# Attention with keys on the partitions: scores computed transposed, row minima from a separate product

## The chip, the cores and the metric

One core of a Trainium2 chip runs the kernel. TensorE (PE in the profile) multiplies matrices into PSUM, VectorE (DVE) and ScalarE (ACT) read PSUM and work elementwise, GpSimd (POOL) works elementwise on SBUF, and SyncE (SP) issues DMAs. Each engine takes its instructions in the order in which they were put in its queue, and waits on semaphores. The metric is the time of one execution on the device in microseconds (us): 4578.61 us is the median of three runs before the change (4577.62 to 4586.95 us).

## The reference, cut to what matters

Two layers. Each has a token mixer (two head groups in parallel: an RWKV-7 recurrence and multi-head latent attention) and a channel mixer. The change touches the attention alone: 8 heads, 1024 latent queries that read all 1280 keys, and, in the first layer only, 256 context queries that read the 256 context keys.

```python
def attend(q, k, v):                      # q, k: 96 features a head; v: 64
    s = jnp.einsum('bqhd,bkhd->bhqk', q, k).astype(F32) * (QK_DIM ** -0.5)
    p = jax.nn.softmax(s, axis=-1).astype(v.dtype)
    return jnp.einsum('bhqk,bkhd->bqhd', p, v)

def mla_latent_attention(q, k_lat, v_lat, k_ctx, v_ctx):
    k_all = jnp.concatenate([k_lat, k_ctx], axis=1)
    v_all = jnp.concatenate([v_lat, v_ctx], axis=1)
    ...
    ob = lax.map(lambda qi: attend(qi, k_all, v_all), qb)   # blocks of 128 queries
```

## The kernel before, in words

The program runs, for each of the two layers: input projections (`in_proj`), the token mixer (`mixer`), the output projection (`out_proj`) and the channel mixer (`ffn`). In the trace the mixers are the stretches from 695 to 1419 us and from 3026 to 3697 us. A Tile scheduler turns the code into one queue for each engine: code that is written earlier has priority, and what is not ready in its plan lets later work pass. So the queues interleave attention and recurrence. What runs on the chip is the fixed queue: an instruction that waits holds up all behind it on its engine.

`mixer` makes ten passes. Each emits a tenth of the attention work, then a chunk of the recurrence (`rwkv_seq` twice, `rwkv_inv2`, `rwkv_prep` for two passes ahead, `rwkv_out`). The recurrence is a chain PE, DVE or ACT, PE, DVE or ACT, with many small products (lines 871 to 1001), and a long run of small DVE instructions that invert triangular blocks (lines 912 and 913).

`attn(l, h, t, first)` computes two heads (h is a pair, e = 0 or 1 within it) for one tile of 128 queries (t). Queries are on the partitions. Its steps:

1. At the first tile of a pair, `raw` keys are loaded and split into a high and a low part (`ka`, lines 1036 and 1037). Each tile's queries are split the same way (`qa`, lines 1044 and 1045).
2. For each head, line 1062 makes the scores `sp` [128 queries, keys] in three PSUM tiles of 512, 512 and 256 keys, each from three products of parts (high x high, high x low, low x high). The tiles' tags s0, s1, s2 have one buffer each.
3. Line 1063 takes the minimum of each tile over the keys, line 1072 that of the three (the scores carry the opposite sign, so the minimum is softmax's maximum). Line 1075 makes P = exp(minimum - score) and its row sums with the accumulator. Lines 1082 and 1083 add the sums and invert them.
4. Keys must be on the partitions for the product with the values. So line 1094 transposes P in blocks of 128x128 into `tp` (four blocks, one buffer), DVE (line 1099) or ACT (line 1097) in turn copies `tp` to `pT`, and line 1104 multiplies with the values `va` into `av`: the two heads of the pair go to two halves of the output partitions. Both are fp32 products. A 128-key block of two heads takes two transposes and two products.
5. Line 1107 spreads the inverted sums over partitions by a product with the identity, and lines 1109 to 1111 scale `av` and store it.

PSUM has eight banks: three for `sp`, one each for `tp` and `av`, three for the recurrence.

## Time and profile before

| | |
|---|---|
| median of 3 runs | 4578.61 us (4577.62 to 4586.95) |
| the profiled execution, its own time | 4579.01 us |
| its span, first to last instruction | 4577.2 us |
| PE, DVE, ACT busy over the span | 4160.3, 2740.3, 1684.0 us |
| mixer of layer 0 (695 to 1419 us): PE, DVE, ACT busy | 635.98, 585.12, 370.07 of 724 us |
| mixer of layer 1 (3026 to 3697 us): PE, DVE, ACT busy | 591.82, 552.13, 337.88 of 671 us |
| granted clock of PE in the mixers; in a stretch of the channel mixer | 0.92 and 0.91; 1.00 |

A busy time is the union of the instructions' durations. A matmul's duration includes its way through the array, in which the next ones already stream, so the time that one costs in a stream is the distance between two starts in a timeline, not its duration. An fp32 matmul that is not a transpose stands in the trace as two instructions (two passes). The granted clock is the share of 2.4 GHz that the throttle let through; its other level is 1.2 GHz.

### The profile page before, as it was taken

The numbers are of one execution on the slowest core, as the hardware profiler recorded it, in microseconds if no ns is written. First come the engines' busy times: TensorE is split into PE (matmuls) and PEld (weight loads), VectorE is DVE, ScalarE is ACT, GpSimd is POOL, SyncE is SP. The second block draws the span as 40 slices with busy tenths as digits, with TensorE's granted clock in tenths as the row PEclk, the third lists the DMA queues.
The fourth block names the chain that finished last, engine by engine and source line by source line (L and its number), as shares of the span: only waits on it lengthen the run. The fifth ranks groups of instructions, "written<-read, shape, count | busy, mean of one in ns | idle before, by whom it ended". The sixth has DMA issues, their size and how long they took to land. (4 is left out here: it accounts for less than half of the span.)

```text
span 4577.2 us, 72936 instructions
## 1 busy us (share of the span) xinstructions
PE 4160.3 (91%) x29598; PEld 3301.1 (72%) x29598; DVE 2740.3 (60%) x4943; ACT 1684.0 (37%) x3000; POOL 543.2 (12%) x492
## 2 busy tenths in 40 slices
PE   8978888899988899999998979888989878999998
PEld 5756666677766788888886856666777656888887
DVE  3225567888886534444447235579888856555456
ACT  3203444544564431221223224464445534222222
POOL 1000000111223300000004000001111244000002
PEclk9989888998999999999998989889998889999999
DMA  6652334323333211111113222343222243111111
GB/s 219 242 174 94 104 120 123 87 66 78 82 77 129 93 39 35 40 40 33 47 35 107 86 72 106 111 142 78 61 72 71 68 135 125 55 51 51 42 51 65
DMA packets 425697, 401.36 MB, mean 88 GB/s; under 512 B 243472, under 2 KB 329936, under 8 KB 425360
## 3 DMA queue, kind: packets, MB, share of 16 engines
q1 hardware_dynamic: 425360, 396.69, 27.9%
q8 instruction: 233, 3.82, 0.3%
q14 instruction: 104, 0.85, 0.1%
HBM read 285.85 MB, written 110.72 MB: 87 GB/s over the span
## 5 line engine op out<-in xcount | busy, mean ns | idle before, releaser
L1266 PE MATMUL up<-u,hi 128*128 128x512 f32 (+1 forms) x3520 | 1012.3, 369 | 3.9 <-ACT hi L1256 3.9
L1266 PEld LDWEIGHTS up<-u,hi 128*128 128x128 f32 x3520 | 643.4, 189 | 119.6 <-ACT hi L1256 4.8
L1266 PE MATMUL up<-u,lo 128*128 128x512 f32 (+1 forms) x1760 | 648.3, 368 | 0.2
L297 PE MATMUL pj<-u,whi 128*128 128x512 f32 (+1 forms) x1888 | 565.9, 384 | 43.4 <-DVE o L318 38.3
L1313 DVE TENSOR_TENSOR acc<-dn,acc 128x512 f32<-128x512 f32 x340 | 233.2, 688 | 431.5 <-PE dn L1307 431.4
L297 PEld LDWEIGHTS pj<-u,whi 128*128 128x128 f32 x1888 | 352.5, 198 | 143.2 <-issue 48.3
L1266 PEld LDWEIGHTS up<-u,lo 128*128 128x128 f32 x1760 | 332.3, 189 | 58.5 <-DVE lo L1258 1.0
L297 PE MATMUL pj<-u,wlo 128*128 128x512 f32 (+1 forms) x944 | 363.5, 385 | 0.1
L1062 PE MATMUL sp<-ka,qa 96*128 96x512 f32 (+1 forms) x1200 | 318.8, 398 | 25.9 <-ACT P L1075 22.2
L1307 PE MATMUL dn<-hi,fh 128*128 128x512 f32 x792 | 311.5, 393 | 7.9 <-ACT fh L1281 4.0
L1256 ACT ACTIVATE hi<-raw 128x512 fp32r<-128x512 f32 x176 | 110.6, 630 | 563.8 <-PE up L1266 560.9
L1307 PE MATMUL dn<-lo,fh 128*128 128x512 f32 x792 | 309.8, 391 | 0.0
L1307 PE MATMUL dn<-hi,fl 128*128 128x512 f32 x792 | 305.6, 390 | 0.0
L1075 ACT ACTIVATE P<-sp,mx 128x512 f32<-128x512 f32 (+1 forms) x400 | 239.4, 606 | 146.3 <-DVE mx L1072 86.7
L1104 PE MATMUL av<-pT,va 128*64 128x128 f32 x2624 | 230.2, 299 | 59.7 <-DVE pT L1099 28.7
L1062 PEld LDWEIGHTS sp<-ka,qa 96*128 96x128 f32 x1200 | 214.6, 204 | 76.5 <-ACT P L1075 32.3
L1063 DVE TENSOR_REDUCE mx<-sp 128x1 f32<-128x512 f32 (+1 forms) x400 | 228.7, 586 | 36.7 <-PE sp L1062 34.7
L1094 PE MATMUL tp<-cst,P 128*128 128x128 f32 x1312 | 234.6, 301 | 7.8 <-ACT P L1075 4.4
L280 ACT ACTIVATE whi<-raw 128x512 fp32r<-128x512 f32 (+2 forms) x110 | 66.1, 603 | 471.7 <-PE pj L297 417.5
L1104 PEld LDWEIGHTS av<-pT,va 128*64 128x64 f32 x2624 | 149.8, 145 | 111.5 <-DVE pT L1099 30.4
L1258 DVE TENSOR_TENSOR lo<-raw,hi 128x512 fp32r<-128x512 f32 x176 | 125.3, 714 | 173.7 <-ACT hi L1256 161.2
L297 PEld LDWEIGHTS pj<-u,wlo 128*128 128x128 f32 x944 | 186.2, 197 | 41.5 <-issue 9.6
(254 smaller groups left out, 7253.5 us busy)
## 6 DMA issues: line engine op xcount, KB each, us to landing
wt<-in_w_ada_dram SPq DMA_DIRECT2D x96, 512.0 KB
raw<-in_w_up_dram SPq DMA_DIRECT2D x176, 256.0 KB
raw<-in_w_down_dram SPq DMA_DIRECT2D x88, 256.0 KB
raw<-in_w_in_dram SPq DMA_DIRECT2D x84, 256.0 KB
bkD<-lt SPq DMA_DIRECT2D x32, 640.0 KB
...
```

The costliest lines, as they stand in the source:

```text
L280: nc.scalar.activation(hi[:, :m], raw[:, :m], AF.Copy)
L297: nc.tensor.matmul(ps[:, o:o + n], ww, u[k][s], start=k == 0 and j == 0, stop=k == nk - 1 and j == 2)
L1062: nc.tensor.matmul(sp[:, o - b0:o - b0 + n], q[:, qq, e], A.k[e][:, kk, o:o + n], start=m == 0, stop=m == 2)
L1063: nc.vector.tensor_reduce(mx[:, i:i + 1], sp[:, :w], axis=AX.X, op=ALU.min)
L1075: nc.scalar.activation(P[:, o:o + w], sp[:, :w], AF.Exp, bias=mn, scale=-1.0, accum_out=mx[:, 4 + i:5 + i])
L1094: nc.tensor.transpose(tp[:, b, e], Ps[e][:, o:o + 128], self.ident)
L1104: nc.tensor.matmul(av[half[e], 0:128], A.v[:, k0 // 128 + kt, half[e]], pT[:, b, e], start=kt == 0, stop=kt == nkt - 1)
L1256: nc.scalar.activation(hi, raw, AF.Copy)
L1258: nc.vector.tensor_tensor(lo, raw, hi, op=ALU.subtract)
L1266: nc.tensor.matmul(ps[:, so:so + sn], ww, uu[k][s], start=k == 0 and m == 0, stop=k == 7 and m == 2)
L1307: nc.tensor.matmul(ps, x[:, t * 128:(t + 1) * 128], w, start=m == 0, stop=m == 3 * len(js) - 1)
L1313: nc.vector.tensor_tensor(dst, ps, dst, op=ALU.add)
```

## The change: what it does

The scores are made a second way round. Work comes in units of 256 queries (`attn(l, h, g)`), and each unit gives two lists of steps:

- `queries` loads and splits 256 queries. `least(t)` makes for 128 queries a first product only (high x high), takes the minimum over the keys, and keeps it (`mn`). `row` turns the four columns of minima into a row by products with the identity (line 1100) and copies it as row 96 of the queries' high part. Row 96 of the keys' high part holds -1 (line 1022).
- `tile(i)` makes with `scores` for one block of 128 keys, keys on the partitions, the transposed scores of both heads (`st`, two buffers; lines 1110 to 1112). The first of the three products runs over 97 rows, so that the minimum is subtracted in PSUM. ACT makes P = exp(-st) with no bias and no accumulator. `values` (of the block before) multiplies P with the values (line 1124) and with a column of ones (line 1127), so that the sums come out spread over 64 partitions. After the last block `close` inverts the sums (a RECIPROCAL over 256 columns), multiplies and stores.

The transposes, the copies of `tp`, the row sums' instructions and the spreading of the inverted sums are gone. `attn_work` weaves the first list of a unit evenly between the steps of the unit before. `attn_keys` loads and splits the keys of a pair through one buffer `raw` (before: three shared with P).

```diff
--- before.py
+++ after.py
@@ -29,7 +29,6 @@
 QK_SCALE = 96 ** -0.5
 C0 = math.exp(-0.5)
 SEGS = [(0, 512), (512, 512), (1024, 256)]
-CUTS = [(0,), (1,), (2,)]
 
 
 PV_CONV = 0
@@ -751,8 +750,7 @@
             self.attn_setup(l, st)
             self.rwkv_setup(l, st)
             need_ctx = l < DEPTH - 1
-            order = ([8, 9] if need_ctx else []) + [3, 4, 2, 5, 1, 6, 0, 7]
-            work = [(h, t) for h in range(NP) for t in order]
+            work = self.attn_work(l)
             done = 0
             self.rwkv_prep(l, 0)
             self.rwkv_inv2(l, 0)
@@ -760,8 +758,8 @@
             for i in range(10):
 
                 upto = len(work) * (i + 1) // 10 if i < 9 else len(work)
-                for h, t in work[done:upto]:
-                    self.attn(l, h, t, t == order[0])
+                for step in work[done:upto]:
+                    step()
                 done = upto
                 self.rwkv_seq(l, i, 0)
                 self.rwkv_seq(l, i, 1)
@@ -1016,99 +1014,135 @@
     def attn_setup(self, l, st):
         tc = self.tc
         A = self.A = Ctx()
-        A.n = 0
         A.p = st.enter_context(tc.tile_pool(name=f"A{l}", bufs=1, reuse_waits="tile"))
-        A.ps = st.enter_context(tc.tile_pool(name=f"As{l}", bufs=1, space=PSUM, reuse_waits="tile"))
         A.pp = st.enter_context(tc.tile_pool(name=f"Ap{l}", bufs=1, space=PSUM, reuse_waits="tile"))
 
-    def attn(self, l, h, t, first):
-
-        nc = self.nc
-        A = self.A
-        p = A.p
-        if first:
-            A.k = []
+        A.k = [A.p.tile([97, 2, NTOK], F32R, name=f"ka{e}") for e in range(2)]
+        for e in range(2):
+            self.nc.scalar.activation(A.k[e][96:97, 0], bc(self.cst[96:97, CO_ONE:CO_ONE + 1], [1, NTOK]), AF.Copy, scale=-1.0)
+
+    def attn_work(self, l):
+
+
+        groups = ([4] if l < DEPTH - 1 else []) + [1, 2, 0, 3]
+        work = []
+        for h in range(NP):
+            units = [self.attn(l, h, g) for g in groups]
+            work.append(lambda h=h: self.attn_keys(l, h))
+            work += units[0][0]
+            for u, (_, tiles) in enumerate(units):
+                ahead = units[u + 1][0] if u + 1 < len(units) else []
+                mixed = [((i + 0.5) / len(v), j, f) for j, v in enumerate((tiles, ahead)) for i, f in enumerate(v)]
+                work += [f for _, _, f in sorted(mixed, key=lambda x: x[:2])]
+        return work
+
+    def attn_keys(self, l, h):
+
+        nc, A = self.nc, self.A
+        for e in range(2):
+            raw = A.p.tile([96, NTOK], F32, name="raw", tag="raw", bufs=1)
+            nc.sync.dma_start(out=raw[0:64], in_=self.kD[l][2 * h + e])
+            nc.sync.dma_start(out=raw[64:96], in_=self.krD[l])
+            k = A.k[e]
+            nc.scalar.activation(k[0:96, 0], raw, AF.Copy)
+            nc.vector.tensor_tensor(k[0:96, 1], raw, k[0:96, 0], op=ALU.subtract)
+        A.v = A.p.tile([128, NTOK // 128, 128], F32, name="va", tag="va")
+        nc.sync.dma_start(out=A.v, in_=self.vD[l][:, :, h * 128:(h + 1) * 128].rearrange("t p x -> p t x"))
+
+    def attn(self, l, h, g):
+
+
+        nc, A = self.nc, self.A
+        p, pp = A.p, A.pp
+        half = [slice(0, 64), slice(64, 128)]
+        kts = list(range(10)) if g < 4 else [8, 9]
+        c = {"P": {}}
+
+        def queries():
+            raw = p.tile([96, 2, 256], F32, name="qr", tag="qr", bufs=1)
+            nc.sync.dma_start(out=raw, in_=self.qD[l][2 * h:2 * h + 2, :, g * 256:(g + 1) * 256].rearrange("h r t -> r h t"))
+            q = c["q"] = p.tile([97, 2, 2, 256], F32R, name="qa", tag="qa", bufs=2)
+            nc.scalar.activation(q[0:96, 0], raw, AF.Copy)
+            nc.gpsimd.tensor_tensor(q[0:96, 1], raw, q[0:96, 0], op=ALU.subtract)
+            c["mn"] = p.tile([128, 2, 2], F32, name="mn", tag="mn", bufs=2)
+
+        def least(t):
+
+            q = c["q"]
+            tok = slice(t * 128, (t + 1) * 128)
+            mx = p.tile([128, 2, 3], F32, name="mx", tag="mx", bufs=4)
+
+            def product(out, e, o, n):
+                nc.tensor.matmul(out, q[0:96, 0, e, tok], A.k[e][0:96, 0, o:o + n], start=True, stop=True)
+
+            n = 0
+            if g < 4:
+                n = 2
+                for e in range(2):
+                    for i in range(2):
+                        sp = pp.tile([128, 512], F32, name="sp", tag="sp", bufs=2)
+                        product(sp, e, 512 * i, 512)
+                        nc.vector.tensor_reduce(mx[:, e, i:i + 1], sp, axis=AX.X, op=ALU.min)
+            sp = pp.tile([128, 2, 256], F32, name="sp", tag="sp", bufs=2)
             for e in range(2):
-                raw = p.tile([128, NTOK], F32, name="raw", tag="P", bufs=3)[0:96]
-                nc.sync.dma_start(out=raw[0:64], in_=self.kD[l][2 * h + e])
-                nc.sync.dma_start(out=raw[64:96], in_=self.krD[l])
...
-            tp = A.pp.tile([128, 2, 2, 128], F32, name="tp", tag="tp", bufs=1)
+                product(sp[:, e], e, 1024, 256)
+            nc.vector.tensor_reduce(mx[:, :, n], sp, axis=AX.X, op=ALU.min)
+            if n:
+                nc.vector.tensor_reduce(c["mn"][:, t], mx, axis=AX.X, op=ALU.min)
+            else:
+                nc.vector.tensor_copy(c["mn"][:, t], mx[:, :, 0])
+
+        def row():
+
+            ps = pp.tile([128, 2, 256], F32, name="mr", tag="sp", bufs=2)
+            for t in range(2):
+                for e in range(2):
+                    nc.tensor.matmul(ps[96:128, e, t * 128:(t + 1) * 128], bc(c["mn"][:, t, e:e + 1], [128, 32]), self.ident,
+                                     start=True, stop=True)
+            nc.scalar.activation(c["q"][96:97, 0], ps[96:97], AF.Copy)
+
+        def scores(kt):
+            q = c["q"]
+            st = pp.tile([128, 2, 256], F32, name="st", tag="st", bufs=2)
+            ks = slice(kt * 128, (kt + 1) * 128)
             for e in range(2):
-                for b in range(2):
-                    o = (kp * 2 + b) * 128
-                    nc.tensor.transpose(tp[:, b, e], Ps[e][:, o:o + 128], self.ident)
...
-        nc.sync.dma_start(out=self.mixD[l][t, :, 4 + h], in_=o1)
+                k = A.k[e]
+                nc.tensor.matmul(st[:, e], k[0:97, 0, ks], q[0:97, 0, e], start=True, stop=False)
+                nc.tensor.matmul(st[:, e], k[0:96, 0, ks], q[0:96, 1, e], start=False, stop=False)
+                nc.tensor.matmul(st[:, e], k[0:96, 1, ks], q[0:96, 0, e], start=False, stop=True)
+
+            P = c["P"][kt] = p.tile([128, 2, 256], F32, name="P", tag="P", bufs=4)
+            nc.scalar.activation(P, st, AF.Exp, scale=-1.0)
+
+        def values(kt):
+
+            if kt == kts[0]:
+                c["av"] = pp.tile([128, 2, 256], F32, name="av", tag="av")
+            av, P = c["av"], c["P"].pop(kt)
+            first, end = kt == kts[0], kt == kts[-1]
+            for e in range(2):
+                nc.tensor.matmul(av[half[e], 0], A.v[:, kt, half[e]], P[:, e], start=first, stop=end, skip_group_check=True)
+            ones = bc(self.cst[:, CO_ONE:CO_ONE + 1], [128, 64])
+            for e in range(2):
+                nc.tensor.matmul(av[half[e], 1], ones, P[:, e], start=False, stop=end, skip_group_check=True)
+
+        def close():
+            av = c["av"]
+            o = p.tile([128, 2, 128], F32, name="o1", tag="o1", bufs=2)
+            of = o.rearrange("p t x -> p (t x)")
+            nc.vector.reciprocal(of, av[:, 1])
+            nc.vector.tensor_tensor(of, av[:, 0], of, op=ALU.mult)
+            nc.sync.dma_start(out=self.mixD[l][2 * g:2 * g + 2, :, 4 + h].rearrange("t p x -> p t x"), in_=o)
+
+        def tile(i):
+            if i < len(kts):
+                scores(kts[i])
+            if i:
+                values(kts[i - 1])
+            if i == len(kts):
+                close()
+
+        return [queries, lambda: least(0), lambda: least(1), row], [lambda i=i: tile(i) for i in range(len(kts) + 1)]
 
 
     def ln_row(self, p, name, src, t=None):
```

The engines' queues, as the builder orders them, at three places. Names: `st` transposed scores, `sp` first products, `mr` the row of minima, `av` value and ones products, `g`, `bt`, `q` products of the recurrence. The changed kernel has line numbers of its own.

PE in the middle of the first mixer, before: scores of one head, then transposes and value products with recurrence between.

```order
L1062 MATMUL sp<-ka,qa 128x256 x3
L971 MATMUL q<-Z,X_4552 64x64 x10
L1104 MATMUL av<-pT,va 64x128 x4
L1094 MATMUL tp<-cst,P 128x128 x4
L971 MATMUL q<-Z,X_4552 64x64 x6
L1104 MATMUL av<-pT,va 64x128 x4
L1094 MATMUL tp<-cst,P 128x128 x4
L816 MATMUL ro<-sq,cst 128x512
L978 MATMUL q<-W,BT 64x64 x12
L1104 MATMUL av<-pT,va 64x128 x4
L1094 MATMUL tp<-cst,P 128x128 x4
```

PE in the middle of the first mixer, changed: one round of the steady state.

```order
L1124 MATMUL av<-P,va 64x256 x2
L1127 MATMUL av<-P,cst 64x256 x2
L1110 MATMUL st<-qa,ka_4540 128x256
L1111 MATMUL st<-qa,ka_4540 128x256
L1112 MATMUL st<-qa,ka_4540 128x256
L1110 MATMUL st<-qa,ka_4541 128x256
L1111 MATMUL st<-qa,ka_4541 128x256
L1112 MATMUL st<-qa,ka_4541 128x256
L1124 MATMUL av<-P,va 64x256 x2
L1127 MATMUL av<-P,cst 64x256 x2
```

A value product stood right behind or right before the transposes of the next block; now it stands behind six score products of the next block, and needs the exponential of the block before that.

PE at the end of a query tile, before: the last products of one tile and the next.

```order
L978 MATMUL q<-W,BT 64x64 x4
L1104 MATMUL av<-pT,va 64x128 x4
L1107 MATMUL av<-cst,mx 64x128 x2
L1094 MATMUL tp<-cst,P 128x128 x4
L996 MATMUL q<-KR,S 64x64 x16
L1001 MATMUL q<-GA,W 64x64 x7
L1104 MATMUL av<-pT,va 64x128 x4
L1094 MATMUL tp<-cst,P 128x128 x4
```

PE at the border between two units, changed: minima's row, last two value steps, first scores of the next unit.

```order
L1100 MATMUL mr<-cst,mn 32x128 x2
L869 MATMUL g<-KR,BK 128x128 x8
L1124 MATMUL av<-P,va 64x256 x2
L1127 MATMUL av<-P,cst 64x256 x2
L1100 MATMUL mr<-cst,mn 32x128 x2
L1124 MATMUL av<-P,va 64x256 x2
L1127 MATMUL av<-P,cst 64x256 x2
L1076 MATMUL sp<-ka_4540,qa 128x512
L879 MATMUL bt<-cst,BK 128x128 x4
L869 MATMUL g<-KR,BK 128x128 x4
L1110 MATMUL st<-qa,ka_4540 128x256
L1111 MATMUL st<-qa,ka_4540 128x256
```

Behind these rows come the scores of four key blocks (24 products) before the next unit's first value product, which needs `av` free.

PE at the end of the first mixer, before.

```order
L1094 MATMUL tp<-cst,P 128x128 x4
L1104 MATMUL av<-pT,va 64x128 x4
L1094 MATMUL tp<-cst,P 128x128 x4
L1104 MATMUL av<-pT,va 64x128 x4
L1107 MATMUL av<-cst,mx 64x128 x2
L1215 MATMUL ps<-hi_13138,mh 128x512
```

PE at the end of the first mixer, changed.

```order
L969 MATMUL q<-Z,X_4553 64x64 x13
L1124 MATMUL av<-P,va 64x256 x2
L1127 MATMUL av<-P,cst 64x256 x2
L969 MATMUL q<-Z,X_4553 64x64 x3
L976 MATMUL q<-W,BT 64x64 x16
L994 MATMUL q<-KR,S 64x64 x16
L999 MATMUL q<-GA,W 64x64 x16
L962 MATMUL q<-W,KR 64x64 x16
L814 MATMUL ro<-sq,cst 128x512
L969 MATMUL q<-Z,X_4553 64x64 x16
L994 MATMUL q<-KR,S 64x64 x16
L999 MATMUL q<-GA,W 64x64 x16
L814 MATMUL ro<-sq,cst 128x512
L1249 MATMUL ps<-hi_12455,mh 128x512
```

Before, attention stood last, with the output projection (line 1215) right behind; now the recurrence's last steps stand alone between the last value product and the output projection (line 1249).

## Rows read from the trace of the kernel before

**Rows 1.** The page of the profile: span, and each engine's busy time.

```profile
span 4577.2 us, 72936 instructions
...
PE 4160.3 (91%) x29598; PEld 3301.1 (72%) x29598; DVE 2740.3 (60%) x4943; ACT 1684.0 (37%) x3000; POOL 543.2 (12%) x492
```

**Rows 2.** Stretches: length, busy PE, PEld, DVE, ACT, POOL, clock, DMA, GB/s.

```profile
695.00:1419.00 724.00, 635.98 (x8059) 499.13 (x8056) 585.12 (x1526) 370.07 (x869) 125.21 (x139) 0.92 0.34 87
3026.00:3697.00 671.00, 591.82 (x7650) 470.53 (x7648) 552.13 (x1456) 337.88 (x798) 108.52 (x121) 0.91 0.31 78
1600.00:2400.00 800.00, 800.00 (x3976) 680.40 (x3975) 377.01 (x477) 189.55 (x216) 0.00 (x0) 1.00 0.13 38
```

**Rows 3.** PE groups: count | busy us, mean ns | idle before <-releasers.

```profile
L1062 PE MATMUL sp<-ka,qa 96*128 96x512 f32 x768 | 248.7, 449 | 21.2 <-ACT P L1075 20.7
L1094 PE MATMUL tp<-cst,P 128*128 128x128 f32 x1312 | 234.6, 301 | 7.8 <-ACT P L1075 4.4 <-ACT pT L1097 2.4 <-DVE pT L1099 0.4
...
L1104 PE MATMUL av<-pT,va 128*64 128x128 f32 x2624 | 230.2, 299 | 59.7 <-DVE pT L1099 28.7 <-ACT pT L1097 17.6 <-DVE mx L1072 5.7
...
L1062 PE MATMUL sp<-ka,qa 96*128 96x256 f32 x432 | 87.6, 307 | 4.7 <-ACT ka L1036 3.0 <-ACT P L1075 1.6
...
L1107 PE MATMUL av<-cst,mx 128*64 128x128 f32 x288 | 30.8, 295 | 0.0
```

**Rows 4.** Timeline of PE, 1013 to 1021 us: start, duration, instructions, count.

```profile
1013.42 0.66 PE L1094 MATMUL tp<-cst,P 128*128 128x128 f32 x4
1013.91 0.60 PE L881 MATMUL bt<-cst,BK 128*128 128x128 f32 x4
...
1015.63 0.66 PE L1104 MATMUL av<-pT,va 128*64 128x128 f32 x8
1016.22 0.66 PE L1094 MATMUL tp<-cst,P 128*128 128x128 f32 x4
1016.80 1.16 PE L871 MATMUL g<-KR,BK 64*128 64x128 f32 x8
...
1019.02 2.01 PE L1062 MATMUL sp<-ka,qa 96*128 96x512 f32 x9
1020.87 0.60 PE L881 MATMUL bt<-cst,BK 128*128 128x128 f32 x4
```

**Rows 5.** Timeline of PE at 1653 us, in the channel mixer.

```profile
1652.88 0.28 PE L1266 MATMUL up<-u,lo 128*128 128x256 f32 x1
1653.00 0.28 PE L1266 MATMUL up<-u,hi 128*128 128x256 f32 x1
```

**Rows 6.** Groups, VectorE and ScalarE, of the attention lines.

```profile
L1063 DVE TENSOR_REDUCE mx<-sp 128x1 f32<-128x512 f32 x256 | 173.8, 683 | 34.1 <-PE sp L1062 32.2
L1075 ACT ACTIVATE P<-sp,mx 128x512 f32<-128x512 f32 x256 | 173.2, 681 | 136.8 <-DVE mx L1072 86.7 <-PE tp L1094 45.6 <-DVE ka L1037 3.5
...
L1099 DVE COPY pT<-tp 128x512 f32<-128x512 f32 x164 | 112.0, 683 | 34.5 <-PE tp L1094 33.4
...
L1097 ACT ACTIVATE pT<-tp 128x512 f32<-128x512 f32 x164 | 97.5, 594 | 92.1 <-PE tp L1094 91.7
...
L1075 ACT ACTIVATION_READ_ACCUMULATOR P<-sp,mx 128x1 f32 x400 | 79.9, 200 | 0.0
...
L1075 ACT ACTIVATE P<-sp,mx 128x256 f32<-128x256 f32 x144 | 67.9, 472 | 9.5 <-DVE mx L1063 7.9 <-PE tp L1094 1.5
...
L1063 DVE TENSOR_REDUCE mx<-sp 128x1 f32<-128x256 f32 x144 | 59.5, 413 | 2.6 <-PE sp L1062 2.5
...
L1083 DVE RECIPROCAL mx<-mx 128x1 f32<-128x1 f32 x144 | 22.4, 155 | 5.9 <-ACT P L1075 4.7
...
L1072 DVE TENSOR_REDUCE mx<-mx 128x1 f32<-128x3 f32 x128 | 18.9, 148 | 1.1
```

**Rows 7.** Timeline of PE at the end of the second mixer.

```profile
3692.70 1.98 PE L996 MATMUL q<-KR,S 64*64 64x64 f32 x32 [3.20 <-DVE W L973]
...
3699.31 1.14 PE L816 MATMUL ro<-sq,cst 128*128 128x512 f32 x2 [2.74 <-ACT sq L814]
```

69 lines of the change are left out of this document (removed).

## The prediction

> **What bounds the kernel now.** I read the page first: PE is busy 91% of the span, DVE 60% [rows 1]. The change is in the two mixers alone, so the second view is busy time by stretch [rows 2]. In the channel mixer PE is busy for all of an 800 us stretch at a clock of 1.00: nothing can be gained or lost there. In the mixers PE is busy 635.98 of 724 and 591.82 of 671 us, so it stands idle for 88 + 79 = 167 us. DVE is busy 81% and 82% of them, and the clock is 0.92 and 0.91, which costs up to 0.08 x 724 + 0.09 x 671 = 118 us. So in 1395 us the bound is PE, with two leaks: waits and a clock that falls with them.
>
> Third, the groups of PE's attention lines show who causes the waits [rows 3]: 21.2 + 4.7 us stood idle ahead of the scores (for exponentials that free their PSUM tile), 59.7 ahead of the value products (for copies of transposed blocks), 7.8 ahead of the transposes. That is 93 of the 167 us; 74 belong to the recurrence's products. Fourth, the timeline of PE gives what one product costs in a stream [rows 4, 5].
>
> **PE's work, before.** Two score runs of nine products (3840 columns each) take 1020.87 - 1019.02 = 1.85 us apiece, 0.48 ns a column [rows 4]. A round of two key blocks takes 0.59 us of value products (1015.63 to 1016.22) and 0.58 of transposes (to 1016.80). Four transposes that no change of tiling follows take 0.49 (1013.42 to 1013.91), so a change of the array's tiling costs 0.09. The spreading of the sums is 30.8 us over 72 tiles, 0.43 each [rows 3]. A tile of 128 queries: 2 x 1.85 + 5 x 1.17 + 0.43 = 9.98 us; 256 queries 20.0.
>
> **PE's work, after, for 256 queries.** Transposed scores: 60 products of 256 columns, 15360 columns as before. That narrow ones cost no more is shown by the channel mixer, 0.12 us for 256 columns [rows 5]; so 7.4 us. Minima: 12 first products, 5120 columns, 2.5 us, new. Values and ones: in each of ten steps four fp32 products of 256 columns into two output halves, twice the columns of the 0.59 us row less its tiling change: 2 x 0.50 + 0.09 = 1.09, and 0.09 back to the scores; 11.8 us. The ones products cost what the transposes did. The minima's row: four small fp32 products, all to the same partitions, so without a partner beside them: 2 x 0.50 and two changes, 1.2 us. Together 22.9: +2.9 us, and for 32 such units +93. The four context units: 5.5 for 4.7 us, +3. PE's work grows by 96 us. Row 97 stays in the same tiling of 128 rows and costs nothing. If every ones product ran without its partner, the term would be 32 x 5 = 160 us more; if the minima's products had partners, 0.5 x 36 = 18 less.
>
> **What other engines lose.** DVE: 164 copies go (112.0 us), 144 inversions (22.4) and as many sums of sums as line 1072 has minima (about 19); 144 minima of 256 columns (59.5) become 72 of 512 (72 x 0.68 = 49) [rows 6]. In come 36 RECIPROCALs of 256 columns. The trace has this operation on one column only, 155 ns. The low bound is a 256-column row, 0.41 us. The high one is eight times the part of that row which grows with columns: 0.41 less 0.15 (the three-column minimum) is 0.26, so 2.1 + 0.15 = 2.3 us. I take 0.41, as the one-column row lies only 7 ns above the three-column minimum. DVE falls from 1137 us by 149 (or 82) to 71% (76%) of the mixers. ACT: 97.5 us of copies and 79.9 of accumulator reads go, 400 exponentials (173.2 and 67.9 us) become 328 at about the 0.59 of a copy of that size, and 36 copies of a row come in: 708 falls to about 505 us [rows 2, 6].
>
> The Trainium skill's VectorE: DVE Perf Modes, in First, the fixed hardware budget, says that the reciprocal runs on iterative divide steps with a repeat count of eight; by it one RECIPROCAL would be an estimated 256 x 8 / 0.96 GHz = 2.1 us and all of them 77. No run here shows it at this size yet; it is the fourth case below.
>
> **Waits, after.** In the changed order six score products (0.74 us) and four value products stand between the scores of a block and the value products that use their exponential, and at most borders more. An exponential takes about 0.6 us [rows 6] against some 1.8 us of cover, where before a copy of 0.68 us had often one group of 0.5 to 0.6 beside it. So the steady state should wait no more. New waits: at each of 36 unit borders the row needs two minima, a product and an ACT copy, of which one value step covers 1.1 us: 0.5 us each, 18. At each of eight pairs' starts the second head's keys now come through the one `raw` buffer, behind the split of the first (an ACT copy and a DVE subtraction), while the minima queue on DVE, ten of 0.68 us: I take 2.5 us of PE idle each after what the recurrence fills, 20 (0 to 8 x 10). SP's queue has the other loads behind that one. So of 93 us 38 stay: -55 (bounds: -93 and +30). The recurrence's 74 us are waits for DVE and ACT copies that queue behind attention's; with 13% less on DVE and 29% less on ACT I take -25 (0 to -45). At the end the recurrence stands alone ahead of the output projection; such an end in the second mixer already shows idle stretches of 3.20 and 2.74 us [rows 7]: +4 each, 8. The clock: where PE never idles it is 1.00, at 12% idle 0.91 to 0.92. Idle halves, so half of 118 us could return; the low stretches lie partly over idle time, so I take -40 (0 to -80).
>
> **Sum.** 96 - 55 - 25 + 8 - 40 = -16 us, against the profiled execution's 4579.01 us, which is 0.4 us above the median: 4563 us. All but the first term are small differences of waits, so its own range is 4530 to 4600. What can be told from no change here is 0.2%, 9 us.
>
> **Rivals.**
>
> Second case, slower: PE is the bound and the new work is simply paid. Its place is the steady state; the price is the 96 us (and 8 at the ends), and it decides as soon as waits and clock return less than 87. For it: PE already streams 88% of the mixers, the minima's products and the row bring nothing that the result needs twice, and the recurrence's waits are its own chain. Against it: 93 us of waits are traced to lines that vanish. Attention's -55 stays, nothing else comes back: 104 - 55 = +49, 4628 us.
>
> Third case, clearly faster: once fed, PE runs as in the channel mixer. Idle falls by 120 of 167, the clock gives 80: 104 - 120 - 80 = -96, 4483 us. For it: the order's cover of 1.8 us, DVE at 71%. Against: the recurrence's chain of PE and DVE steps remains, and the clock is low today in stretches of small products also.
>
> Fourth, the slow RECIPROCAL: 36 x (2.3 - 0.41) = 68 us more of DVE, and `av` has one buffer, so the next unit's value products wait for it; the order puts four blocks' scores (3.0 us) there, which covers 2.3 + 0.4 us on PE, but the recurrence's copies queue behind it: about half reaches PE, +34 on the forecast, 4597 us.
>
> **How the numbers follow.** Forecast 0.36, second 0.33, third 0.23, fourth 0.08. Of the forecast's range about six tenths lie under 4570, a quarter within 9 us of the median, the rest above. Faster: 0.22 + 0.23 = 0.45; same: 0.09 + 0.01 + 0.02 = 0.12; slower: 0.05 + 0.31 + 0.07 = 0.43. The range reaches to both outer cases and a little beyond the dearer one, as unpaired ones products and pair starts have bounds on that side: 4475 to 4660.
>
> **What would show it.** Right: four value and ones products in about 1.09 us; score runs of six in 0.74; PE idle ahead of lines 1110 and 1124 under 40 us in all; DVE near 71% of the mixers; a clock of 0.94 or more there; mixers of about 715 and 664 us. Wrong: idle ahead of the value products that names line 1089 or 1133 (minima or the close) as releaser; ones products that start one after the other, 0.2 us apart; a clock that stays at 0.91 with less idle; RECIPROCAL near 2 us; or a recurrence that lags and makes the end of a mixer longer than 20 us without attention.

## The result and the profile after

The changed kernel takes 4698.22 us (median of 4 runs, 4693.94 to 4709.77) against 4578.11 us before (median of 4 as well): 1.028 times as long by the comparison of the runs, 95% interval 1.0258 to 1.0306; the two medians alone give 1.026. The forecast was 4563 us with a range to 4660: the sign and the range are both wrong. The profiled execution took 4700.59 us.

The page of the changed kernel, to be held against [rows 1]:

```profile
span 4698.7 us, 71166 instructions
...
PE 4297.3 (91%) x29454; PEld 3336.6 (71%) x29454; DVE 2686.1 (57%) x4379; ACT 1546.2 (33%) x2296; POOL 533.5 (11%) x456
```

DVE and ACT fell, as they should; PE is busy 137 us longer. Busy time by stretch, to be held against the first two of [rows 2]: each mixer from its first to its last attention product, then from there to the first product of the output projection (columns as in [rows 2]):

```profile
707.00:1447.00 740.00, 679.26 (x7730) 499.58 (x7728) 540.72 (x1211) 273.23 (x467) 107.21 (x107) 0.91 0.29 72
3112.00:3788.00 676.00, 636.67 (x7310) 470.32 (x7308) 510.03 (x1165) 253.69 (x437) 94.30 (x95) 0.91 0.28 70
1447.00:1495.00 48.00, 15.80 (x229) 12.56 (x229) 15.74 (x22) 17.23 (x23) 9.88 (x8) 0.59 0.40 113
3788.00:3840.00 52.00, 17.49 (x263) 13.94 (x262) 18.39 (x25) 18.41 (x25) 10.46 (x8) 0.60 0.44 124
```

Both mixers with their ends take 788 + 728 = 1516 us. Before they took 724 + 691 = 1415: in the first mixer the output projection followed the last attention product at once, in the second 28 us later, so that the second mixer before, with its end, is this row:

```profile
3026.00:3717.00 691.00, 593.00 (x7653) 470.87 (x7651) 554.87 (x1461) 344.29 (x805) 113.85 (x125) 0.90 0.31 80
```

So 101 of the 122 us by which the span grew lie in the mixers; 22 more come from mixers that begin 12 and 10 us later after the stage before. In the mixers PE is idle for 167 us where it was idle for 186, and it is busy for 1349 us where it was busy for 1229.

The attention itself did what was forecast. Its groups on PE (as in [rows 3]):

```profile
L1124 PE MATMUL av<-P,va 128*64 128x256 f32 x1312 | 225.7, 407 | 7.1 <-ACT P L1115 5.0 <-DVE o L1134 2.1
...
L1110 PE MATMUL st<-qa,ka 97*128 97x256 f32 x656 | 216.5, 330 | 6.9 <-ACT qa L1102 5.1 <-ACT P L1115 1.7
...
L1076 PE MATMUL sp<-ka,qa 96*128 96x512 f32 x256 | 118.1, 504 | 15.6 <-DVE mx L1085 6.7 <-DVE mx L1089 4.6 <-ACT ka L1047 3.9
...
L1100 PE MATMUL mr<-cst,mn 128*32 128x128 f32 x288 | 51.8, 314 | 4.4 <-DVE mn L1091 2.2 <-DVE mn L1093 1.1 <-DVE mx L1085 1.1
L1076 PE MATMUL sp<-ka,qa 96*128 96x256 f32 x144 | 37.2, 344 | 8.3 <-ACT ka L1047 6.6 <-DVE mx L1085 1.7
```

The idle times ahead of them sum to 42 us, where 38 were forecast in place of 93. One step of a stream, in PE's timeline:

```profile
1431.32 0.39 PE L1110 MATMUL st<-qa,ka 97*128 97x256 f32 x1
...
1432.24 0.65 PE L1124 MATMUL av<-P,va 128*64 128x256 f32 x4
1432.72 0.60 PE L1127 MATMUL av<-P,cst 128*64 128x256 f32 x4
1433.25 0.39 PE L1110 MATMUL st<-qa,ka 97*128 97x256 f32 x1
```

From scores to scores are 1.93 us; the forecast's 0.74 + 1.09 + 0.09 are 1.92. What went wrong shows at the end of the first mixer, in PE's timeline:

```profile
1446.02 0.60 PE L1127 MATMUL av<-P,cst 128*64 128x256 f32 x4
1446.56 0.44 PE L969 MATMUL q<-Z,X 64*64 64x64 f32 x6
1451.53 1.98 PE L976 MATMUL q<-W,BT 128*64 128x64 f32 x32 [4.53 <-DVE W L971]
...
1462.38 2.04 PE L962 MATMUL q<-W,KR 128*64 128x64 f32 x32 [4.11 <-DVE ysb L1006]
...
1472.93 1.97 PE L994 MATMUL q<-KR,S 64*64 64x64 f32 x32 [5.27 <-DVE W L971]
...
1494.99 1.22 PE L1249 MATMUL ps<-hi,mh 128*128 128x512 f32 x2 [15.70 <-ACT mh L1208]
```

The attention is through, and PE goes from one link of the recurrence to the next, 4 to 5 us of waiting apiece; then the output projection waits 15.70 us for the recurrence's last rows to be stored, loaded and split. The same happens in the second mixer. Before, the recurrence was through with its products 27 us ahead of the attention in the first mixer, and its own end in the second was 28 us long.

The twenty steps of the recurrence (line 962, before line 964) show it in figures. In the first mixer the first step begins at 815.31 and the last at 1462.38, 34.1 us a step; before it was 790.09 and 1371.02, 30.6. In the second mixer 31.8 in place of 29.6. The starts, in PE's timelines, the changed kernel's first (its last stands above), then the two of the kernel before:

```profile
815.31 1.15 PE L962 MATMUL q<-W,KR 128*64 128x64 f32 x32
...
790.09 1.15 PE L964 MATMUL q<-W,KR 128*64 128x64 f32 x32
...
1371.02 0.80 PE L964 MATMUL q<-W,KR 128*64 128x64 f32 x18
```

One way in which a step loses time is seen in one place of the changed kernel. DVE's timeline, the copy that the next product needs:

```profile
1035.24 0.68 DVE L964 COPY Z<-q 128x512 f32<-128x512 f32 x1
```

and PE's at the same time:

```profile
1036.04 0.38 PE L1110 MATMUL st<-qa,ka 97*128 97x256 f32 x1
...
1036.95 0.65 PE L1124 MATMUL av<-P,va 128*64 128x256 f32 x4
1037.43 0.60 PE L1127 MATMUL av<-P,cst 128*64 128x256 f32 x4
1037.96 0.39 PE L1110 MATMUL st<-qa,ka 97*128 97x256 f32 x1
...
1038.76 1.15 PE L969 MATMUL q<-Z,X 64*64 64x64 f32 x32
```

Z is ready at 1035.92; its product starts at 1038.76, behind one and a half steps of attention that never stop. PE is not idle for a moment, and the recurrence has lost 2.84 us. Over all steps the two waits of this kind (Z's copy to line 969, W's copies to line 976) come to 3.5 and 3.9 us a step in the two mixers, where they were 1.4 and 2.0 before. That is more than half of the steps' own growth, but it is not yet the cause: the run without reductions, below, has the same waits and shorter steps.

### The profile page after: what moved, and what is told of

It is laid out like the page before. It is cut to its first block, busy times and chain, and to the rows that moved or that the text cites. A ratio compares the mean times of both kernels' runs of the same rounds, so it can differ in the third digit from the quotient of the medians.

```text
span 4698.7 us, 71166 instructions
## 1 busy us (share of the span) xinstructions
PE 4297.3 (91%) x29454; PEld 3336.6 (71%) x29454; DVE 2686.1 (57%) x4379; ACT 1546.2 (33%) x2296; POOL 533.5 (11%) x456
## 5 line engine op out<-in xcount | busy, mean ns | idle before, releaser
L1115 ACT ACTIVATE P<-st 128x512 f32<-128x512 f32 x328 | 194.6, 596 | 327.1 <-PE st L1112 317.6
L1124 PE MATMUL av<-P,va 128*64 128x256 f32 x1312 | 225.7, 407 | 7.1 <-ACT P L1115 5.0
L1110 PE MATMUL st<-qa,ka 97*128 97x256 f32 x656 | 216.5, 330 | 6.9 <-ACT qa L1102 5.1
L1127 PE MATMUL av<-P,cst 128*64 128x256 f32 x1312 | 217.5, 388 | 0.0
L1085 DVE TENSOR_REDUCE mx<-sp 128x1 f32<-128x512 f32 x256 | 170.6, 682 | 69.9 <-PE sp L1076 69.0
L911 DVE TENSOR_TENSOR T<-T,tmp 128x126 f32<-128x126 f32 (+22 forms) x620 | 196.4, 317 | 16.5
L910 DVE TENSOR_TENSOR tmp<-Dt,T 128x126 f32<-128x126 f32 (+22 forms) x620 | 190.7, 308 | 16.0
```

The lines of the kernel that those rows point to most:

```text
L910: eng.tensor_tensor(tv, bc(Dt[:, j + 1:, j:j + 1], [128, r, w]), bc(T[:, j:j + 1, :w], [128, r, w]), op=ALU.mult)
L911: eng.tensor_tensor(T[:, j + 1:, :w], T[:, j + 1:, :w], tv, op=ALU.subtract)
L1085: nc.vector.tensor_reduce(mx[:, e, i:i + 1], sp, axis=AX.X, op=ALU.min)
L1110: nc.tensor.matmul(st[:, e], k[0:97, 0, ks], q[0:97, 0, e], start=True, stop=False)
L1115: nc.scalar.activation(P, st, AF.Exp, scale=-1.0)
L1124: nc.tensor.matmul(av[half[e], 0], A.v[:, kt, half[e]], P[:, e], start=first, stop=end, skip_group_check=True)
```

## Experiments

The theory at first was that the recurrence, written behind the attention, is now left for the end (theory T); its rivals were that PE's added work is simply paid (P), and later that the recurrence's own chain sets the length (L), held up on DVE (D) or on PE (Q).

The table holds what the traces of the main runs show for both mixers together, from the first mixer product to the output projection (PE's clock: first and second mixer).

| kernel | time, ratio to before | mixers | PE busy | PE idle | clock | after the last attention product |
|---|---|---|---|---|---|---|
| before | 1 | 1415 | 1229 | 186 | 0.92, 0.90 | 0, 28 |
| changed | 1.0282 | 1516 | 1349 | 167 | 0.89, 0.89 | 48, 51 |
| e1_seq_first | 1.0181 | 1481 | 1341 | 140 | 0.90, 0.89 | 0, 55 |
| e3_no_minima | 0.9892 | 1359 | 1175 | 184 | 0.90, 0.89 | 147, 133 |
| e6_pool_sum | 1.0441 | 1598 | 1298 | 300 | 0.84, 0.79 | 111, 112 |
| e7_no_attention | 0.951 | 1152 | 726 | 426 | 0.59, 0.59 | |
| e8_no_rec_after | 0.8924 | 905 | 815 | 90 | 0.90, 0.90 | |
| e9_no_rec_before | 0.8985 | 933 | 728 | 205 | 0.91, 0.96 | |
| e10_q2 | 1.0585 | 1677 | 1510 | 167 | 0.85, 0.86 | 0, 0 |
| e14_no_reduce | 1.0031 | 1395 | 1275 | 120 | 0.95, 0.93 | 47, 58 |
| e19_no_reduce_seq | 0.9972 | 1384 | 1273 | 111 | 0.94, 0.93 | 31, 80 |

### Is it the recurrence's place in the order?

```diff
             for i in range(10):
+                self.rwkv_seq(l, i, 0)
+                self.rwkv_seq(l, i, 1)
                 upto = len(work) * (i + 1) // 10 if i < 9 else len(work)
...
-                self.rwkv_seq(l, i, 0)
-                self.rwkv_seq(l, i, 1)
```

> The changed kernel with one edit: in each pass of the mixer the two recurrence steps are written ahead of the pass's attention chunk instead of behind it, so the scheduler prefers them. Theory T (the end): the recurrence was pushed behind the attention and the 49 and 52 us without attention at the ends of the two mixers are its price. It expects these ends below 15 us each, the attention's part of the mixers (751 and 686 us) longer by the recurrence's PE work that moves into it (some 17 us each) and no more, and 4630 us (4610 to 4650) in place of 4698. Theory P (PE is the bound and the new products are simply paid): the time lies in the attention's part; moving the recurrence changes less than 20 us, 4680 to 4700. Theory L (the recurrence's own chain is the limit): its steps come no earlier, attention waits for nothing, the ends stay above 35 us.

4660.07 us, 1.0181 (1.0155 to 1.0206): 38 us less, half of theory T's gain. The first mixer's end is gone; the second's stays:

```profile
3744.00:3799.00 55.00, 16.97 (x262) 13.61 (x260) 19.09 (x25) 19.28 (x27) 9.94 (x8) 0.61 0.41 118
```

Its steps still take 31.3 us. The kernel before with the same edit:

> The kernel before with the same edit (recurrence steps written ahead of the attention chunk). Theory T: the transposing attention left holes on PE through which the recurrence kept up, so here the edit has little to win: the ends without attention are near 0 and 28 us, and the time falls by 0 to 25 us, 4553 to 4578. Rival (the order of the recurrence is worth the same in both kernels): 55 to 75 us less, 4503 to 4523.

4582.99 us, 1.0015 (1.0000 to 1.0030): nothing gained, 5 us above the upper end of theory T's range and far from its rival's 55 to 75 us. Then the whole recurrence of a pass was written ahead:

```diff
+                upto = len(work) * (i + 1) // 10 if i < 9 else len(work)
+                for step in work[done:upto]:
+                    step()
+                done = upto
                 # moved here, behind inv2, prep and the outputs of the pass
```

> The changed kernel with the whole recurrence of a pass (its two steps, the next inverse and the preparation of the pass after that) written ahead of the pass's attention chunk, where the run before moved the two steps alone and left 55 us at the end of the second mixer. Theory T (priority): now the recurrence is never behind in the second mixer either; both ends fall below 10 us, 4600 to 4630. Theory L (the recurrence's own chain, each link of which waits on PE's queue behind a run of attention, is the second limit and no order of writing shortens it much): the twenty steps still take 590 us or more in each mixer, the second mixer's end stays above 35 us, and the time is 4640 to 4670.

4661.62 us, 1.0211 (1.0186 to 1.0236), no better than e1; the ends are 7 and 48 us and the steps 31.8 and 31.4 us. Theory T falls short and theory L's three numbers hold: the recurrence is not only late because others were preferred.

### Each part alone

```diff
-            work = self.attn_work(l)
+            work = []
```

> The changed kernel with the attention left out (zeros are stored in its place), so that the recurrence stands alone in both mixers. Theory L: its chain alone is long: from its first product to the output projection 560 to 640 us in each mixer (passes of 50 to 60 us as in the end of the run without minima), while PE is busy under 40% of it. Theory P (the mixers are bound by PE's work, and the recurrence is a filler): under 450 us a mixer.

4343.35 us. The recurrence alone, both mixers by stretch:

```profile
713.00:1302.00 589.00, 371.63 (x5237) 317.32 (x5238) 401.53 (x975) 163.30 (x277) 92.82 (x95) 0.59 0.30 75
2917.00:3480.00 563.00, 354.61 (x5008) 305.43 (x5008) 385.88 (x954) 153.12 (x265) 85.03 (x89) 0.59 0.30 73
```

It is no filler: by itself it takes 589 and 563 us, with steps of 26.0 and 24.9 us (theory L's length; PE is busy 63% of it and not under 40%). The granted clock is 0.59 here, so the length is that of the chain at a low clock; at the mixers' 0.9 it was not measured. In the next two runs the recurrence is left out:

```diff
-                self.rwkv_seq(l, i, 0)
-                self.rwkv_seq(l, i, 1)
-                if i < 9:
-                    self.rwkv_inv2(l, i + 1)
...
```

> The changed kernel with the recurrence left out (zeros are stored in its place), so that its attention stands alone. By the streams in the trace (391 and 366 us) and 42 us of waits the attention alone takes 400 to 430 and 375 to 405 us, at a clock of 0.95 or more. Theory P: the change's cost is here: 50 us or more above the attention alone of the kernel before, over both mixers. Theory L: the attention alone is no slower than before's by more than 20 us over both mixers, and faster if its clock is higher; what the change costs comes with the recurrence beside it.

> The kernel before with the recurrence left out (zeros stored in its place). By the streams in its trace (342 and 327 us) and 93 us of waits, 385 to 420 and 365 to 400 us. If its waits were those of the attention alone, PE is idle 12% here and its clock lies below 0.95; if they came from the recurrence's copies on DVE and ACT, PE is idle less than 5% and the attention alone takes 345 to 370 and 330 to 355 us (theory P then has its 50 us and more).

4075.81 us (0.8924, 0.8890 to 0.8958) for the changed attention, 4103.70 us (0.8985, 0.8950 to 0.9020) for the one before. Both are longer than either expectation, and the new one's clock is 0.90 where 0.95 was expected; but before's waits are its own (PE is idle for 22% of it, where 12% were the mark), and theory L has the comparison right. The two intervals touch, with two runs of each; the mixers in the traces say the same with 905 against 933 us, 28 less. The changed attention alone, and in the last six rows a border between two pairs of heads:

```profile
699.00:1169.00 470.00, 419.99 (x2740) 278.39 (x2741) 178.70 (x275) 143.80 (x237) 23.66 (x18) 0.90 0.16 48
2781.00:3216.00 435.00, 394.97 (x2576) 260.52 (x2576) 166.71 (x250) 135.17 (x221) 28.79 (x18) 0.90 0.17 51
...
799.00:809.00 10.00, 8.95 (x66) 5.57 (x65) 2.49 (x2) 4.07 (x6) 1.56 (x1) 1.00 0.03 9
809.00:819.00 10.00, 0.86 (x3) 0.60 (x4) 4.07 (x7) 1.27 (x1) 0.00 (x0) 0.57 0.60 145
819.00:829.00 10.00, 9.32 (x40) 6.22 (x42) 2.75 (x5) 2.30 (x4) 1.27 (x1) 0.57 0.16 44
829.00:839.00 10.00, 6.90 (x28) 3.97 (x25) 6.62 (x12) 0.59 (x1) 0.00 (x0) 0.77 0.12 34
839.00:849.00 10.00, 10.00 (x56) 6.61 (x56) 2.74 (x5) 2.39 (x4) 0.00 (x0) 0.72 0.01 2
849.00:859.00 10.00, 10.00 (x71) 6.43 (x72) 3.43 (x6) 2.99 (x5) 0.00 (x0) 1.00 0.00 0
```

and the attention before alone:

```profile
692.00:1186.00 494.00, 383.93 (x2821) 274.93 (x2820) 230.15 (x566) 226.21 (x610) 27.86 (x38) 0.91 0.16 50
2790.00:3229.00 439.00, 344.35 (x2648) 247.10 (x2646) 220.36 (x521) 209.72 (x557) 32.17 (x34) 0.96 0.17 54
```

This is the centre of the case. Alone, the change costs PE 87 us of busy time (815 for 728; some of it is the clock, 0.90 against 0.91 and 0.96) and saves 115 us of waiting (90 for 205): a gain of 28. The kernel before does two parts of 933 and 1152 us in 1415 us, 670 less than their sum; the changed one does 905 and 1152 in 1516, 541 less. The 1152 stands in both sums, so the 129 us of overlap that went are the loss of the mixers, 101, and the 28 that the attention gained by itself: the whole loss comes with the recurrence beside the attention. That the recurrence used to run in the holes that the change closed is the reading that suggests itself; these runs do not show it, and the run without reductions, below, tells against it as the whole cause.

### Is it PE's work, or what waits for the minima?

> The changed kernel without its minima: their products, DVE minima and the row's products and copy are left out, the 97th row is a constant zero, and the exponential's argument is scaled by 1/128 so that it stays finite. Left out on PE: 256 products of 512 columns at 0.22 us and 144 of 256 at 0.12, 73 us, and 36 rows at 1.2, 43 us; the waits ahead of them, 28 us (15.6, 8.3, 4.4). Theory P (all of PE's work is paid): 144 us less, 4555. Theory T: the attention's part falls by as much, but the recurrence does not come earlier and the ends grow above 52 us: 4570 to 4620. If the minima were hidden: over 4660.

```diff
-        return [queries, lambda: least(0), lambda: least(1), row], [...]
+        return [queries], [...]
```

4526.42 us, 0.9892 (0.9867 to 0.9917): 172 us less, more than all of the 144 us on PE. The attention then ends 147 and 133 us before the mixers do, so the recurrence's chain, with steps of 28.7 us, is all that is left to wait for. The opposite test takes work from PE alone:

```diff
-            for e in range(2):
-                nc.tensor.matmul(av[half[e], 1], ones, P[:, e], start=False, stop=end, skip_group_check=True)
+            if first:
+                c["P0"] = P
+            elif "sum" not in c:
+                c["sum"] = p.tile([128, 2, 256], F32, name="ps", tag="ps", bufs=1)
+                nc.gpsimd.tensor_tensor(c["sum"], c["P0"], P, op=ALU.add)
+            else:
+                nc.gpsimd.tensor_tensor(c["sum"], c["sum"], P, op=ALU.add)
```

> The changed kernel with the exponentials' sums taken by POOL adds of the 128x512 tiles and spread by one pair of ones products at the end of a unit, in place of a pair in each of its ten steps. PE loses some 290 runs of four ones products at 0.54 us, 157 us. Theory P (PE's work is the bound): all of it comes back, 4530 to 4550, and the ends without attention stay near 50 us. Theory L (the recurrence's chain is the bound, and waits behind attention's runs on PE): the attention's parts shorten by 150 us or more together, but the recurrence gains only what its links wait less behind steps of 1.3 in place of 1.8 us; its twenty steps take 28 to 30 us each, the ends without attention grow above 80 us, 4540 to 4600. If POOL's adds hold back DVE or the values, 4640 or more.

4782.30 us, 1.0441 (1.0392 to 1.0490): 84 us more. Both theories missed; the last case of the expectation, POOL's adds holding back DVE (4640 or more), is what came. The attention's parts did shorten, from 740 and 676 us only to 688 and 687, and the ends grew to 111 and 112 us. The reason is on DVE, which had nothing added. The recurrence's inverse there, in the changed kernel

```profile
L911 DVE TENSOR_TENSOR T<-T,tmp 128x126 f32<-128x126 f32 x60 | 22.3, 372 | 1.4
```

and with POOL at work beside it

```profile
L911 DVE TENSOR_TENSOR T<-T,tmp 128x126 f32<-128x126 f32 x60 | 31.4, 524 | 1.6
```

The same instruction takes 524 ns in place of 372, and 318 with no attention at all. The inverse's instructions on `tmp`, 620 in each mixer, keep DVE busy for 271 and 266 us, where it was 196 and 191. The inverse is part of the recurrence's chain; the steps take 34.3 and 33.7 us. PE had 1298 us busy in place of 1349, and the mixers took 82 us longer; as the edit slowed DVE, this neither proves nor refutes theory P, that PE's work is the bound. What POOL does to the rest of the chain was not separated.

Then the minima were taken apart. First their products stay, and the reductions go:

```diff
-                        nc.vector.tensor_reduce(mx[:, e, i:i + 1], sp, axis=AX.X, op=ALU.min)
...
-            nc.vector.tensor_reduce(mx[:, :, n], sp, axis=AX.X, op=ALU.min)
...
-            nc.scalar.activation(c["q"][96:97, 0], ps[96:97], AF.Copy)
+            nc.scalar.activation(c["q"][96:97, 0], ps[96:97], AF.Copy, scale=0.0)
```

> The changed kernel with its minima's products and the row's products left on PE, and the DVE reductions behind them left out (the row is zero, the exponential's argument is scaled by 1/128). The run without any minima took 172 us less. Theory D (the recurrence's links wait in DVE's queue, behind reductions of 0.68 us): most of that comes back here, 4540 to 4590, and steps of the recurrence fall below 30 us. Theory Q (they wait in PE's queue, behind attention's products): 4660 to 4700, steps of 32 to 34 us.

4588.13 us, 1.0031 (1.0014 to 1.0048): 110 of the 172 us, inside theory D's range at its upper end and far from theory Q's. Its stretches:

```profile
708.00:1378.00 670.00, 636.97 (x7731) 473.55 (x7729) 441.19 (x1004) 273.11 (x468) 109.27 (x111) 0.97 0.32 79
1378.00:1425.00 47.00, 15.89 (x229) 12.66 (x230) 15.19 (x22) 16.64 (x22) 10.53 (x8) 0.65 0.43 122
3041.00:3662.00 621.00, 601.02 (x7278) 448.82 (x7276) 408.25 (x967) 250.58 (x435) 92.68 (x94) 0.96 0.30 73
3662.00:3719.00 57.00, 20.69 (x292) 16.85 (x292) 20.39 (x29) 19.77 (x28) 12.00 (x10) 0.56 0.48 137
```

The products on PE are those of the changed kernel, and PE is busy for 1275 us in place of 1349: in the attention's parts the clock is 0.97 and 0.96 in place of 0.91. Idle time falls by another 46 us. So what waits for the minima costs more than their products: 46 us by itself and 75 in busy time, with the higher clock. Theory P, that the added products are simply paid, is refuted here: PE has all its products, and 110 us come back.

The steps take 30.6 and 29.0 us, the first not below theory D's 30, and nearly those of the kernel before (30.6 and 29.6). Yet the two waits on PE, for Z's product and for that of W, are 3.6 and 3.8 us a step, as in the changed kernel (3.5 and 3.9). So these waits in PE's queue alone do not make the steps long; other links became shorter with the reductions gone, and which ones was not separated. The ends stay at 47 and 58 us, as the attention became shorter too.

The products are what is left between this run and the one without any minima, 62 us. The other half was meant to say the same from the other side:

> The opposite half: the minima's and the row's products and the row's copy are left out, and as many DVE reductions of the same size run on a constant (the row is zero, the exponential's argument is scaled by 1/128). Theory D: 4650 to 4700. Theory Q, and theory P (PE's work is the bound): 4530 to 4590. Where each of the two halves gives about half of the 172 us, recurrence and attention share both queues and no single one is the bound.

```diff
-                        product(sp, e, 512 * i, 512)
-                        nc.vector.tensor_reduce(mx[:, e, i:i + 1], sp, axis=AX.X, op=ALU.min)
+                        nc.vector.tensor_reduce(mx[:, :, i], bc(self.cst[:, None, 0:256], [128, 2, 256]), axis=AX.X, op=ALU.min)
```

4642.55 us, 1.0138 (1.0109 to 1.0167), 56 us less. This run separates little: reductions that wait for no product ran early and stood ahead of the recurrence's first inverse. Its first step began 151 and 148 us after the mixer (changed kernel 108 and 88, without minima 100 in both), and 99 of the 116 us that it takes longer than the run without minima are there. Whether the 110 us are due to DVE's time or to the path from product over reduction and row to the scores stays open.

Last, both costs in one kernel:

> The run without DVE reductions (110 us less) and the recurrence's steps written first (38 us less) in one kernel. If the two costs are separate, the reductions' queue and the recurrence's place at the end, the gains add to 4545 to 4560, below the kernel before, as the attention by itself is 27 us faster. If the steps' place matters only because the reductions delay them, the second edit brings less than 15 us more here: 4575 to 4590.

4564.70 us, 0.9972 (0.9958 to 0.9986). Moving the steps brings 23 us here (38 with the reductions in place), between the two expectations: the recurrence's place and the wait for the minima look like two costs that overlap in part. Without the reductions the changed order beats the kernel before by 0.3%, where the changed attention alone is 28 us faster than the one before; but a kernel needs its minima.

### Attempts to make the recurrence faster

One PSUM bank was moved from the minima to the recurrence:

```diff
-            R.pq = st.enter_context(tc.tile_pool(name=f"Rq{l}", bufs=1, space=PSUM, reuse_waits="tile"))
+            R.pq = st.enter_context(tc.tile_pool(name=f"Rq{l}", bufs=2, space=PSUM, reuse_waits="tile"))
...
-                        sp = pp.tile([128, 512], F32, name="sp", tag="sp", bufs=2)
+                        sp = pp.tile([128, 512], F32, name="sp", tag="sp", bufs=1)
```

> The changed kernel with one PSUM bank moved from attention's minima (sp, two buffers to one) to the recurrence's chain (q, one buffer to two), so that a step's output products need not be copied out before the next step begins. Theory L: each of twenty steps loses 3 to 5 us of its 34 and 32 us, the ends without attention fall below 30 us, 4560 to 4640. Theory P: the chain is not the bound; the minima that now wait for one another cost PE 0 to 40 us, 4690 to 4740.

> The same moved bank, and the recurrence's two steps written ahead of the pass's attention chunk (the first run's edit). Theory L: both gains on one chain, not quite their sum: 4540 to 4620, steps of 27 to 29 us. Theory P: as the first run, 4655 to 4690.

> The moved bank, the steps written first and the sums on POOL together. Theory L: with the chain shorter and attention's steps at 1.3 us the mixers take some 600 to 640 us each, 4420 to 4500, faster than the kernel before. Theory P: the sums' 157 us alone, 4500 to 4540.

4844.06 us (1.0585, 1.0553 to 1.0617), 4897.25 us (1.0697, 1.0661 to 1.0734) and 4972.02 us (1.0863, 1.0823 to 1.0903; with the sums on POOL as in e6). Every one is far on the wrong side of theory L's cure. Stretches of e10:

```profile
708.00:1576.00 868.00, 775.79 (x7960) 563.68 (x7959) 560.50 (x1233) 290.93 (x491) 119.08 (x113) 0.85 0.28 71
3186.00:3995.00 809.00, 734.28 (x7568) 533.61 (x7568) 532.02 (x1188) 271.90 (x463) 107.91 (x105) 0.86 0.27 71
```

and a piece of its timeline on PE:

```profile
1288.84 0.91 PE L969 MATMUL q<-Z,X 64*64 64x64 f32 x22
1289.68 1.16 PE L869 MATMUL g<-KR,BK 64*128 64x128 f32 x8
1290.77 0.56 PE L969 MATMUL q<-Z,X 64*64 64x64 f32 x10
...
1292.83 0.33 PE L976 MATMUL q<-W,BT 128*64 128x64 f32 x2
```

A link's 32 products are now cut by others in the middle more often: the 189 links (lines 962 to 999) of both mixers stand in 505 pieces, where the changed kernel has 245 and the one before 263. PE passes between attention and recurrence 1098 times in both mixers, where it did so 624 times in the changed kernel and 737 in the one before, and is busy 161 us more with the same products at a clock of 0.85 and 0.86; now the attention is what ends last. How much of that is the cutting and how much the minima's single buffer was not separated.

Smaller edits. The inversion of the sums on ACT:

```diff
-            nc.vector.reciprocal(of, av[:, 1])
+            nc.scalar.activation(of, av[:, 1], AF.Ln)
+            nc.scalar.activation(of, of, AF.Exp, scale=-1.0)
```

> The changed kernel with the 36 RECIPROCALs of 128x256 (1748 ns each, 62.9 us of DVE) replaced by a logarithm and an exponential on ACT (some 0.6 us each). Theory R (the slow RECIPROCAL reaches PE through av's one buffer and the recurrence's queued copies, for half of it): 25 to 40 us less, 4660 to 4673. Theory T: within 12 us of the changed kernel, 4686 to 4710, as the order puts 3 us of scores over it; the ends without attention stay at 45 to 55 us.

4688.91 us, 1.0248 (1.0219 to 1.0276): within theory T's 12 us; the interval overlaps that of the changed kernel. Four copies of the chain on ACT, in the changed kernel (with the edits of e1 and e4) and in the one before:

```diff
-        nc.vector.tensor_copy(Z, ps)
+        nc.scalar.activation(Z, ps, AF.Copy)
...
-        nc.vector.tensor_scalar(W[half[1], 1], ps[half[1]], -1.0, None, op0=ALU.mult)
+        nc.scalar.activation(W[half[1], 1], ps[half[1]], AF.Copy, scale=-1.0)
```

> The changed kernel with the recurrence's steps written ahead of the chunk, the inversion of the sums on ACT, and four copies of the recurrence's chain (Z, the second half of W, the two halves in the inverse) moved from DVE to ACT, which the change left at a third of its time. Theory D: the waits ahead of these copies (1.7 us for Z) fall to 0.5 and a step by 2 us, 4570 to 4620. Theory Q: as the runs with one of the edits, 4640 to 4665. W's halves now follow each other on one engine, 0.6 us more a step: if that and ACT's exponentials decide, 4670 or more.

> The kernel before with the same four copies moved to ACT. There ACT also copies the transposed blocks and DVE is at 81%: theory D expects 20 to 50 us less, 4525 to 4560; theory Q no change, 4565 to 4590; if W's halves in sequence decide, 4600 or more.

4651.31 us (1.0165, 1.0141 to 1.0189) and 4566.20 us (0.9977, 0.9961 to 0.9993). They lie 31 and 6 us above what theory D expected and within theory Q's ranges: which engine copies is a small matter here, and the waits of these copies in DVE's queue are not the larger part of what e14 took away, as far as an edit shows it that also puts W's halves one after the other. Of the forms of the changed kernel that still compute everything this has the lowest median, 4651 us, with an interval that overlaps that of e1; it does not beat the kernel before, which itself gains 0.2% by its four copies.

```diff
-            self.nc.scalar.activation(A.k[e][96:97, 0], bc(...), AF.Copy, scale=-1.0)
+            self.nc.gpsimd.tensor_scalar(A.k[e][96:97, 0], bc(...), -1.0, None, op0=ALU.mult)
```

> The changed kernel with the keys' constant 97th row (two copies of 1x1280, 2.42 us on ACT) written by POOL instead. In the changed kernel these stand in ACT's queue ahead of a copy of the stage before, for which PE waits 4.92 us where it waited 1.49, and the first attention product of the mixers starts at 707.0 and 3111.9 us, 12 and 10 us later after the stage before than in the kernel before. If that queue is the cause of the later start: 5 to 15 us less, 4680 to 4692. If the two splits of keys and the single raw buffer are: within 5 us of 4698.

4693.68 us, 1.0248 (1.0222 to 1.0275). The medians differ by 5 us, the bound between the two answers, and its mixers begin at 705.2 and, 1618 us after the first one's end, at 3094.2, where the changed kernel had 707.0 and 1617. The later start is not settled by it.

## Why the prediction was wrong

PE's work: right in size. Forecast +96 us; alone the attention's PE time grew by 87, part of it clock. A step of the stream is 1.93 us for the forecast 1.92, with some luck: its scores take 0.92 for 0.83 (1431.32 to 1432.24), as a change of tiling costs on both sides, its value and ones products 1.01 for 1.09.

Attention's waits: right in size. 42 us stand ahead of its groups in the changed kernel, 38 were forecast. Alone it even gained 28 us, where these two terms and the clock's add up to 1 us lost.

The clock: wrong, "I take -40", and the largest part of the miss. It stayed at 0.91 in the attention's parts, though PE's idle share there fell from 12% to 8 and 6%, and with the ends it is 0.89 in both mixers, where it was 0.92 and 0.90. Of the 100 us that PE still stood idle in the attention's parts, 42 are ahead of attention's products, most of them at borders of units and pairs, and 58 ahead of the recurrence's. The changed attention alone shows PE busy for 0.86 of 10 us at a border of pairs, and the granted clock between its two levels (1.2 and 2.4 GHz), 0.57 to 0.77 of the upper one, over the 40 us from 809. With the reductions left out the clock rose to 0.97 and 0.96 and the same products took 75 us less: the forecast's term was there to be had, but not in this kernel. Which of the waits holds the clock down was not separated.

The recurrence: wrong, and with the clock the step that failed. "The recurrence's 74 us are waits for DVE and ACT copies that queue behind attention's; with 13% less on DVE and 29% less on ACT I take -25", and "at the end the recurrence stands alone ahead of the output projection ... +4 each, 8". Both treat it as work that fills PE and waits for other engines. By itself, at a clock of 0.59, it needs 1152 us, against 1415 for both parts together, and less work on DVE and ACT did not hasten it: its steps grew by 3.5 and 2.3 us, and 48 and 51 us at the ends stand alone, at a clock of 0.59 and 0.60, where 0 and 28 did. The waits ahead of two of its links on PE grew by 2.1 and 1.9 us a step, but they are as long without the reductions, with steps of 30.6 and 29.0 us. What makes the steps longer goes with the reductions of the minima; whether through DVE's queue, through the path from the product to the scores, or through the clock stays open.

In sums for the mixers, which name the terms by their size: PE's busy time rose by 120 us where 56 were forecast (96 less 40), 64 too few; idle time at the ends grew by some 45 where 8 were forecast (32 and 35 us, against 22 before), 37 too few; elsewhere it fell by 64 where 80 were forecast, 16 too few. With the 22 us of later starts, for which the forecast had no term, these are 139 us, to be held against the 138 between 4563 and the profiled 4700.59.

The rivals: none is what happened. The second, that PE's work is simply paid, came nearest with 4628 us, but its mechanism is refuted by the run without reductions, in which PE has all its products and 110 us come back; that its number is near is luck. The fourth had its price: RECIPROCAL does take long,

```profile
L1133 DVE RECIPROCAL o<-av 128x256 f32<-128x256 f32 x36 | 62.9, 1748 | 6.5 <-PE av L1127 6.2
```

1.75 us and not the 0.41 that was taken. The Trainium skill's VectorE: DVE Perf Modes, First, the fixed hardware budget, with its repeat count of eight was the better guide here (estimate 2.1 us). The trace lies below it: 1748 ns less the 155 of one column [rows 6] are 6.2 ns for each of the other 255, about six cycles at the 0.96 GHz that the page states. But taking it off DVE left the median 9 us lower, with intervals that overlap, so this is no visible part of the failure. The text's own list of what would make it wrong named "a recurrence that lags and makes the end of a mixer longer than 20 us without attention": that row was the right one to watch, and it had been given no chance.
